# Where a kernel makes the token sums for a fast matrix product: in the convolution stage, or inside the two merges that come later

## The chip, the cores and the metric

One core of one Trainium2 chip. Five engines work on it side by side, each through its own instructions in order: TensorE (PE, matmuls; PEld is its weight load), VectorE (DVE), ScalarE (ACT), GpSimd (POOL) and SyncE (SP). DMAs are issued from the queues of SP, POOL and ACT. The metric is the device time of one execution, in microseconds (us); lower is better.

## The reference, cut to what matters

The program is one step of a backbone for 2048 sample tokens and 128 prompt tokens of width 1024. One input projection feeds three branches: A (short convolution on q, k, v, then a gated DeltaNet scan in both directions), B (spatial gating) and C (Fourier mixing). Each branch is projected to the model's width and multiplied by a sigmoid gate that is itself a projection of the same tokens; the three products are added, projected once more and added to the tokens.

```python
proj = jnp.einsum('btd,de->bte', xn, w_in)
qkv, beta, dec, z_a, u_b, v_b, z_b, x_c, z_c, gates = jnp.split(proj, points, axis=-1)
qkv = short_conv(qkv, conv_w).astype(jnp.float32)
...
br = jnp.stack([o_a, o_b, o_c], axis=2)
pb = jnp.einsum('btnw,nwd->btnd', br, w_branch)
gt = jax.nn.sigmoid(gates.reshape(B, T, N_BRANCH, D_MODEL))
merged = jnp.einsum('btnd,btnd->btd', gt, pb)
return jnp.einsum('btd,de->bte', merged, w_out), s_f, s_b
```

## The kernel before, in words

**Numbers.** Every matrix is held as two 16-bit parts, a high and a low one (`whi`, `wlo`; `x` has both in one tile), and a product is three matmuls that add in one PSUM bank. `mm`, the helper that records every matmul, is line 161, so nearly all matmuls have that line. The normalised tokens stay in SBUF as four quarters, `XQ` (`x_4` to `x_7` in the lists of instructions), plus `xp` for the prompt.

**Weights.** A block of 128 columns is read into one of two staging buffers `wst` (line 195, queue of SP), squared on ACT for its scale (L209), the sum cast on DVE (L175, `wscb`) and spread over the partitions by a small matmul with `ones`; DVE makes the scale from it (L183 to L187, `winv` L220), ACT writes the high part (L222) and DVE the low part (L223), which frees the staging buffer. A list `wlist` holds the order; `getw` and `weight_step` walk through it ahead of use.

**Stages.** First the tokens are normalised and transposed and `z_a` is projected. Then comes the convolution stage: twelve column blocks of q, k and v (`ct`), each a projection of all tokens in five pieces (four of 512, one of 128), copied by ACT into `raw` (L784), three passes of DVE over 2178 columns (L793 to L795), a sigmoid on ACT and a product on POOL (L799). Beside it run the decays of the scan (`decays`, DVE L584 to L624, then L689 and L690 per chunk; its loads are L673 on SP's queue). From the seventh block on, two weights a block are needed, as `w_out` and `w_branch` are converted and stored too (`keep`, L752). Behind it come the branches B and C, with the scan's preparation and the scan itself beside them, and then three merges: branch B (`merge(1, ...)`), branch C (`merge(2, ...)`) and branch A (`last_merge`).

**The merges.** `merge` goes through eight column blocks (`db`), each in two halves of the tokens (`h0` = 0 with two pieces, `h0` = 1024 with three). A piece is the gate's product (24 matmuls of 512 columns), its sigmoid on ACT into a buffer `sg` (L1530), the branch's product (12 matmuls) and their product on DVE (L1536, or L1539 in the second merge, where POOL then adds the row of the merge before, L1540). The scan's steps are interleaved: copies into T and R on POOL (L1022, L1024), key products on POOL (L1128, L1131), and splits into two 16-bit parts on ACT and DVE (L1065, L1066).

**The token sums.** The last merge's gate products use a scheme that needs fewer products, and it takes sums and differences of the token quarters in their place. `token_sums` (lines 701 to 738) makes them: for each of 2 x 4 parts of the tokens four steps, each of which makes one result. `whole` (L717, POOL) adds the two parts of a token quarter into a buffer `sg`; L723, L730 and L734 (DVE) and L727 (POOL) add and subtract; `pair_out` splits the result again into a buffer `st`, high part on ACT (L708), low part on DVE, or POOL for the fourth step (L709), and POOL's queue stores it (L711), two steps late. There are four buffers `sg` and three `st`; the merges take their `sg` from the same four. The four results go to DRAM (`xs`, 8.4 MB) and are read back by the last merge alone.

Before, 12 of the 32 steps are taken in the first three convolution blocks, one behind each piece of 512 tokens, and 20 behind the loop over the blocks.

**What sets the order.** The program is written as a stream of instructions, and a scheduler then sorts the instructions of each engine by priority (the order of writing, except where `high_priority` lifts one) and by a timeline of its own. So an instruction that is written later can stand earlier, and one edit changes the order in many places.

## Time and profile before

| | us |
|---|---|
| median of three runs | 2239.32 (2233.18 to 2240.04) |
| the profiled execution | 2242.02 |
| its span, first to last instruction | 2240.2 |
| PE busy | 2134.1 (95%) |
| DVE busy | 1443.1 (64%) |
| ACT busy | 1047.8 (47%) |
| POOL busy | 827.7 (37%) |
| mean granted clock of PE | 0.984 |

Busy time counts an engine's instructions, not its waits, nor the issue of DMAs from its queue. A row of a view of groups reads: line, engine, operation, what it writes <- what it reads, shapes, count, busy time, mean of one in ns, then the engine's idle time just before these instructions and who ended it. A row of the order of time reads: start, duration, then the same names, and in brackets the idle time before and who ended it. A row of waits reads: who waited for whom, total, times, the longest. "PEq", "SPq" and so on are an engine's queue.

### The profile page before, as it was taken

What the parts mean: (1) busy time and instruction counts of PE and PEld (TensorE: products, weight loads), DVE (VectorE), ACT (ScalarE), POOL (GpSimd) and SP (SyncE); (2) the same over time, 40 slices, a digit from 0 to 9 for tenths busy, and PEclk for the clock granted to TensorE, in tenths of its full rate; (3) what the DMA queues carried; (4) which work ended last, traced back from release to release, by engine and by line L of the source; (5) the groups of instructions that cost most, each with busy time, mean ns of one, the idle gap of its engine ahead of it and who ended that gap; (6) DMA issues with size and microseconds to landing.
All of it is one profiled execution on the core that took longest, in us unless ns stands there. A gap on an engine that the chain in (4) does not pass through costs nothing. (4 is left out here: it accounts for less than half of the span.)

```text
span 2240.2 us, 42450 instructions
## 1 busy us (share of the span) xinstructions
PE 2134.1 (95%) x15878; PEld 1227.4 (55%) x15878; DVE 1443.1 (64%) x3250; ACT 1047.8 (47%) x2394; POOL 827.7 (37%) x972
## 2 busy tenths in 40 slices
PE   7998978999899999899999999999999999999998
PEld 3564433445555567788755565565555445444443
DVE  5748989558888877735565555675565455444553
ACT  3634754546565656334464444665554332222331
POOL 1445467322243332233312232345453323433443
PEclk9999989999999999999999999999999999999999
DMA  8423944448787765424475555676664856564542
GB/s 273 159 83 119 313 158 148 145 134 253 230 289 227 215 199 154 106 83 143 130 223 172 161 167 175 201 231 207 202 204 153 255 165 201 179 223 149 167 142 86
DMA packets 333625, 404.94 MB, mean 181 GB/s; under 512 B 41345, under 2 KB 240106, under 8 KB 330602
## 3 DMA queue, kind: packets, MB, share of 16 engines
q1 hardware_dynamic: 311114, 327.36, 48.1%
q0 software_dynamic: 15248, 59.66, 7.3%
q10 hardware_dynamic: 7056, 15.21, 1.8%
q8 instruction: 125, 2.05, 0.4%
q14 instruction: 82, 0.67, 0.1%
HBM read 259.83 MB, written 142.30 MB: 180 GB/s over the span
## 5 line engine op out<-in xcount | busy, mean ns | idle before, releaser
L161 PE MATMUL b<-x,whi 128*128 128x512 f16 x3008 | 908.2, 382 | 5.5 <-DVE sg L1539 2.5
L161 PE MATMUL b<-x,wlo 128*128 128x512 f16 x1504 | 574.2, 382 | 0.0
L161 PEld LDWEIGHTS <-whi 128*128 128x128 f16 x3776 | 346.5, 98 | 338.1 <-issue 35.6
L161 PEld LDWEIGHTS <-wlo 128*128 128x128 f16 x1888 | 185.6, 98 | 180.7 <-issue 13.8
L161 PE MATMUL b<-big,bhi 128*128 128x512 f16 (+1 forms) x960 | 251.7, 348 | 2.9 <-ACT big L1500 1.5
L161 PE MATMUL b<-big,blo 128*128 128x512 f16 (+1 forms) x480 | 163.4, 348 | 0.0
L161 PEld LDWEIGHTS <-x 128*128 128x128 f16 x2176 | 131.3, 98 | 43.6 <-issue 4.2
L161 PEld LDWEIGHTS <-bhi 128*128 128x128 f16 x960 | 86.8, 98 | 74.9 <-issue 3.7
L161 PE MATMUL b<-x,m 128*128 128x512 f16 x528 | 114.8, 379 | 0.0
L799 POOL TENSOR_TENSOR cy<-cy,raw 128x545 f32<-128x545 f32 (+1 forms) x48 | 72.4, 1547 | 109.6 <-ACT raw L798 109.6
L1022 POOL COPY T<-ES 32x256 f16<-32x256 f16 x68 | 31.4, 462 | 208.1 <-DMA ES<-ei 202.5
L209 ACT ACTIVATE wlo<-wst 128x1024 f16<-128x1024 f32 (+1 forms) x64 | 64.2, 1003 | 93.6 <-DMA wst<-in_w_in_dram 64.0
L223 DVE SCALAR_TENSOR_TENSOR wlo<-wst,wsc,whi 128x1024 f16<-128x1024 f32 (+1 forms) x64 | 91.1, 1426 | 19.3 <-ACT whi L222 18.8
L222 ACT ACTIVATE whi<-wst,wsc 128x1024 f16<-128x1024 f32 (+1 forms) x64 | 69.7, 1093 | 64.2 <-DVE wsc L186 57.9
L161 PE MATMUL b<-whi,x 128*128 128x128 f16 x1024 | 90.7, 219 | 0.0
L1128 POOL TENSOR_TENSOR skn<-skn,ed 128x512 f32<-128x512 f32 x34 | 36.3, 1067 | 144.8 <-DMA skn<-kv 128.5
L175 DVE CAST wscb<-wss 128x1 bf16<-128x1 f32 x101 | 15.3, 152 | 111.9 <-ACT wlo L209 74.3
L161 PE MATMUL b<-wlo,x 128*128 128x128 f16 x512 | 87.4, 219 | 0.0
L161 PEld LDWEIGHTS <-m 128*128 128x128 f16 x528 | 51.1, 98 | 61.4
L161 PE MATMUL b<-x,zhi 128*128 128x512 f16 x256 | 78.7, 383 | 0.1
L161 PE MATMUL b<-v4hi,x 128*128 128x512 f16 x256 | 78.5, 383 | 0.1
L1660 POOL TENSOR_TENSOR mrow<-mrow,sg 128x512 f32<-128x512 f32 (+1 forms) x40 | 46.5, 1165 | 82.2 <-DVE sg L1659 73.9
(483 smaller groups left out, 4475.6 us busy)
## 6 DMA issues: line engine op xcount, KB each, us to landing
wst<-in_w_in_dram SPq DMA_DIRECT2D x56, 512.0 KB, 4.7
qkv<-cy POOLq DMA_DIRECT2D x12, 1089.0 KB, 5.7
st<-br SPq DMA_DIRECT2D x48, 256.0 KB, 3.5
mrow<-mrg SPq DMA_DIRECT2D x16, 576.0 KB, 4.5
mrg<-mrow POOLq DMA_DIRECT2D x16, 576.0 KB, 3.7
dc<-dec SPq DMA_DIRECT2D x17, 512.0 KB, 4.6
kq<-qkv SPq DMA_DIRECT2D x34, 256.0 KB, 4.2
kv<-tok POOLq DMA_DIRECT2D x17, 512.0 KB, 5.6
```

What stands on the lines that cost most here:

```text
L161: PE.matmul(out, l, r, start=start, stop=stop)
L175: V.tensor_copy(sb16, ss)
L209: A.activation(w.lo, st, AF.Square, accum_out=ss)
L222: w.made = A.activation(w.hi, st, AF.Copy, scale=s)
L223: V.scalar_tensor_tensor(w.lo, st, s, w.hi, ALU.mult, ALU.subtract)
L799: G.tensor_tensor(y[:, c0:c1], y[:, c0:c1], raw[:, 1 + c0:1 + c1], ALU.mult)
L1022: G.tensor_copy(T16[rows(a0, b), :, :, b], ES[0:32, :, 2 * a0 + b, :, wT])
L1128: G.tensor_tensor(h3(kn_), h3(kn_), bc(ed[:, d, t, :], P), ALU.mult)
L1660: G.tensor_tensor(mr, mr, sg, ALU.add)
```

## The change

The calls of the token sums in the convolution stage go, both the one behind a piece and the loop behind the blocks. In their place `merge` takes four steps, which is one whole part, before the second half of column blocks 1 to 4, in both of its calls: 2 x 4 x 4 = 32 steps. The two stores that are still owed at the end are issued behind the second merge.

```diff
                 pace.tick(tn / 100)
-                if ct < 3 and tn == 512:
-                    next(sums)
                 if ct > 4:
                     weight_step()
...
     pace.drain()
-    with tc.issue_after(dlast[0].ins):
-        for _ in sums:
-            pass
     a1.close()
...
                 if each is not None and (n == 0 or db > 3):
                     next(gates, 0)
+                if h0 and 0 < db < 5:
+                    for _ in range(4):
+                        next(sums)
                 for t0, tn in tbs:
...
     inv_ = merge(2, False, inv_, finish_delta, then=(0, 17))
+    for _ in sums:
+        pass
     cs_.close()
```

Lines behind the first edit have numbers two lower in the changed program, those behind the second five lower, and those behind the third two lower again; from the last merge on they are the same.

DVE at the decays, at the start of the convolution stage. `tok` holds the decays; `sg` and `st` are the sums' buffers. Before:

```order
L597 TENSOR_SCALAR tok_1779<-tok_1779 128x136
L598 RECIPROCAL tok_1779<-tok_1779 128x136
L730 TENSOR_TENSOR sg_2147<-sg_2091,sg_2147 128x512
L709 TENSOR_TENSOR st_2150<-sg_2089,st_2150 128x512
L599 TENSOR_TENSOR tok_1779<-tok_1779 128x136
L600 TENSOR_SCALAR tok_1779<-tok_1779 128x136
L601 TENSOR_TENSOR tok_1779<-tok_1779 128x136
L602 TENSOR_TENSOR tok_1779<-tok_1779 128x136
L709 TENSOR_TENSOR st_2196<-sg_2147,st_2196 128x512
L734 TENSOR_TENSOR sg_2243<-sg_2243,sg_2147 128x512
L603 SCALAR_TENSOR_TENSOR tok_1779<-tok_1779 128x136
L610 SCALAR_TENSOR_TENSOR tok_1779<-tok_1779,al_1783 128x68 x2
```

Now:

```order
L597 TENSOR_SCALAR tok_1779<-tok_1779 128x136
L598 RECIPROCAL tok_1779<-tok_1779 128x136
L599 TENSOR_TENSOR tok_1779<-tok_1779 128x136
L600 TENSOR_SCALAR tok_1779<-tok_1779 128x136
L601 TENSOR_TENSOR tok_1779<-tok_1779 128x136
L602 TENSOR_TENSOR tok_1779<-tok_1779 128x136
L603 SCALAR_TENSOR_TENSOR tok_1779<-tok_1779 128x136
L610 SCALAR_TENSOR_TENSOR tok_1779<-tok_1779,al_1783 128x68 x2
```

Four instructions of the sums have left the chain of the decays, whose last row PE's prefix sums read.

DVE at about the seventh and eighth column block, between the low part of one weight (L223) and the cast of the next (L175). `cy` is the convolution. Before:

```order
L220 TENSOR_TENSOR winv_2957<-wsc_2952,xsc_305 128x1
L223 SCALAR_TENSOR_TENSOR wlo_2917<-wst_2875,wsc_2952,whi_2916 128x1024
L730 TENSOR_TENSOR sg_4208<-sg_4201,sg_4208 128x512
L709 TENSOR_TENSOR st_4211<-sg_4199,st_4211 128x512
L734 TENSOR_TENSOR sg_4220<-sg_4220,sg_4208 128x512
L793 TENSOR_SCALAR cy_3015<-raw_2845,pc_111 128x2178
L175 CAST wscb_3062<-wss_3060 128x1
L794 SCALAR_TENSOR_TENSOR cy_3015<-raw_2845,pc_111,cy_3015 128x2178
L709 TENSOR_TENSOR st_4216<-sg_4208,st_4216 128x512
L723 TENSOR_TENSOR sg_4229<-sg_4227,sg_4229 128x512
L795 SCALAR_TENSOR_TENSOR cy_3015<-raw_2845,pc_111,cy_3015 128x2178
```

Now:

```order
L220 TENSOR_TENSOR winv_2875<-wsc_2870,xsc_305 128x1
L223 SCALAR_TENSOR_TENSOR wlo_2835<-wst_2793,wsc_2870,whi_2834 128x1024
L791 TENSOR_SCALAR cy_2933<-raw_2763,pc_111 128x2178
L175 CAST wscb_2980<-wss_2978 128x1
L792 SCALAR_TENSOR_TENSOR cy_2933<-raw_2763,pc_111,cy_2933 128x2178
L793 SCALAR_TENSOR_TENSOR cy_2933<-raw_2763,pc_111,cy_2933 128x2178
```

The five instructions of the sums are gone; the rest stands in the same order.

POOL in the first merge, where the first group comes in. `skn`, `kn`, T and R belong to the scan, `x_4` to `x_7` are the token quarters. Before:

```order
L1131 TENSOR_TENSOR kn_1874_14145<-skn_14111,kn_1874_14145 128x512
L1128 TENSOR_TENSOR skn_14393<-skn_14393,ed_1399 128x512
L1022 COPY T_1513_10755<-ES_10761 32x8x32 x2
L1024 COPY R_1512_10753<-ES_10761 32x8x32 x4
L1131 TENSOR_TENSOR kn_1909_14427<-skn_14393,kn_1909_14427 128x512
L1128 TENSOR_TENSOR skn_14689<-skn_14689,ed_1399 128x512
```

Now:

```order
L1123 TENSOR_TENSOR skn_14195<-skn_14195,ed_1399 128x512
L717 TENSOR_TENSOR sg_14154<-x_4_93 128x512
L717 TENSOR_TENSOR sg_14156<-x_5_94 128x512
L717 TENSOR_TENSOR sg_14162<-x_6_95 128x512
L1017 COPY T_1449_10531<-ES_10537 32x8x32 x2
L1019 COPY R_1448_10529<-ES_10537 32x8x32 x4
L727 TENSOR_TENSOR sg_14154<-sg_14162,sg_14154 128x512
L717 TENSOR_TENSOR sg_14173<-x_7_96 128x512
L711 DMA xs_1436<-st_14159 256x1x512
L1126 TENSOR_TENSOR kn_1853_14229<-skn_14195,kn_1853_14229 128x512
L711 DMA xs_1438<-st_14165 256x1x512
L711 DMA xs_1437<-st_14169 256x1x512
```

Three sums now stand ahead of the copies into T and R, and two more, with a store, ahead of the key product (L1126, before L1131); each waits for a free `sg`.

## The prediction, made before the changed kernel was run

> **What bounds the kernel now.** On the page TensorE (PE) is the busiest engine in nearly every slice of the span, so time can come only from the stretches in which it stands still or runs slowly. I read the waits of PE over the whole run first, then the busy times by stage. Around the change there are two places: the convolution stage, from which the token sums leave (about 150 to 448 us), and column blocks 1 to 4 of the first two merges, into which they go. Busy times of the convolution stage (stretch, length, then PE, PEld, DVE, ACT, POOL busy with counts, granted clock, DMA share, GB/s), and PE's waits in it:
>
> ```profile
> 150.00:213.00 63.00, 55.86 (x566) 32.38 (x564) 45.88 (x57) 23.89 (x43) 38.90 (x45) 0.95 0.37 117
> 213.00:287.00 74.00, 74.00 (x418) 36.43 (x416) 70.81 (x63) 53.63 (x68) 29.40 (x27) 1.00 0.78 266
> 287.00:396.00 109.00, 86.28 (x427) 39.67 (x426) 101.77 (x97) 54.73 (x86) 76.77 (x85) 0.91 0.44 150
> 396.00:448.00 52.00, 51.07 (x296) 25.48 (x296) 28.36 (x54) 28.61 (x42) 13.08 (x19) 1.00 0.47 151
> ...
> PE b L161 <- DVE wscb L175: 23.6, 6, 8.2
> PE b L161 <- DVE tok L610: 7.1, 1, 7.1
> ```
>
> The token sums run in the first and third stretch. In the second and fourth, which do the same convolution without them, PE is busy 74.00 of 74 and 51.07 of 52 us. In the third PE lacks 22.7 us while DVE is busy 101.77 of 109 us and POOL 76.77; in the first it has one hole of 7.1 us. Every wait named is one on a small DVE instruction: the cast that starts a weight's scale (L175), and the last step of the decays (L610).
>
> Idle time is not the whole loss, because PE comes back slow. Two pairs of rows of PE's order of time, before and behind the hole at 179 us, and the matmuls of 287 to 396 us by shape:
>
> ```profile
> 178.30 0.59 PE L161 MATMUL b<-x,whi 128*128 128x512 f16 x2
> 178.73 0.38 PE L161 MATMUL b<-x,wlo 128*128 128x512 f16 x1
> ...
> 188.36 0.63 PE L161 MATMUL b<-x,wlo 128*128 128x512 f16 x1
> 188.79 0.63 PE L161 MATMUL b<-x,whi 128*128 128x512 f16 x1
> ...
> L161 PE MATMUL b<-x,whi 128*128 128x512 f16 x232 | 74.0, 401 | 0.0
> L161 PE MATMUL b<-x,wlo 128*128 128x512 f16 x116 | 46.3, 399 | 0.0
> L161 PE MATMUL b<-xp,whi 128*128 128x128 f16 x48 | 4.3, 219 | 0.0
> L161 PE MATMUL b<-xp,wlo 128*128 128x128 f16 x24 | 4.2, 219 | 0.0
> ```
>
> Before the hole two matmuls start within 0.43 us, 0.215 each; behind it one start takes 0.43. At 0.215, the 348 long matmuls and the 72 short ones (a quarter of the columns, 18 long ones) need 366 x 0.215 = 79 us. The stretch took 109: **30 us lost**. Behind the 7.1 us hole, some 4 us at half speed lose 2 more: **9 us**.
>
> **What the change takes out.** How a late cast comes about, by the order of time on DVE, POOL, SP and ACT:
>
> ```profile
> 306.38 4.44 DVE L752 TENSOR_TENSOR oinv<-winv,xsc 128x1 f32<-128x1 f32 x1
> 310.71 1.35 POOL L717 TENSOR_TENSOR sg<-x 128x512 f32<-128x512 f16 x1
> 310.75 5.81 DVE L223 SCALAR_TENSOR_TENSOR wlo<-wst,wsc,whi 128x1024 f16<-128x1024 f32 x1
> 311.82 2.44 POOL L799 TENSOR_TENSOR cy<-cy,raw 128x545 f32<-128x545 f32 x2
> 316.59 0.38 SPq L195 DMA_DIRECT2D wst<-in_w_out_dram  x1
> 320.45 1.06 ACT L209 ACTIVATE wlo<-wst 128x1024 f16<-128x1024 f32 x1 [0.30 <-DMA wst<-in_w_out_dram]
> 325.23 0.14 DVE L175 CAST wscb<-wss 128x1 bf16<-128x1 f32 x1
> ...
> 395.44 0.16 DVE L752 TENSOR_TENSOR oinv<-winv,xsc 128x1 f32<-128x1 f32 x1
> 395.52 1.28 DVE L223 SCALAR_TENSOR_TENSOR wlo<-wst,wsc,whi 128x1024 f16<-128x1024 f32 x1
> ```
>
> L752 and L223 took 10.3 us here and take 1.44 when POOL leaves them alone (395.44, 395.52). L223 frees the weight's staging buffer, so the next read is issued only at 316.59, its square ends at 321.5, and the cast then stands behind sums and a convolution until 325.23: PE's 8.2 us hole. Without sums this chain is about 9 us earlier, and the cast has less ahead of it. The work that leaves, grouped over 150 to 410 us:
>
> ```profile
> L709 DVE TENSOR_TENSOR st<-sg,st 128x512 f16<-128x512 f32 x24 | 28.1, 1180 | 1.8 <-ACT st L708 1.8
> L734 DVE TENSOR_TENSOR sg<-sg,sg 128x512 f32<-128x512 f32 x8 | 10.6, 1321 | 0.0
> L730 DVE TENSOR_TENSOR sg<-sg,sg 128x512 f32<-128x512 f32 x8 | 10.4, 1300 | 1.2 <-POOL sg L727 1.2
> L723 DVE TENSOR_TENSOR sg<-sg,sg 128x512 f32<-128x512 f32 x8 | 7.3, 918 | 3.9 <-POOL sg L717 3.9
> ...
> L717 POOL TENSOR_TENSOR sg<-x 128x512 f32<-128x512 f16 x32 | 46.4, 1452 | 8.7 <-DVE sg L730 4.9 <-DVE wsc L183 2.1 <-DMA sz<-sg 1.6
> L711 POOL DMA_DIRECT2D xs<-st x30 | 21.2, 714 | 26.6 <-DVE st L709 11.5 <-DVE wsc L183 7.5 <-DVE wscb L175 2.1
> L727 POOL TENSOR_TENSOR sg<-sg,sg 128x512 f32<-128x512 f32 x8 | 11.9, 1486 | 2.8 <-DVE sg L723 2.8
> L709 POOL TENSOR_TENSOR st<-sg,st 128x512 f16<-128x512 f32 x8 | 10.8, 1344 | 5.2 <-ACT st L708 5.2
> ...
> L708 ACT CAST st<-sg 128x512 f16<-128x512 f32 x32 | 19.5, 614 | 37.7 <-DMA xs<-st 18.3 <-DVE sg L734 9.6 <-issue 3.7
> ```
>
> That is 56.4 us of DVE, 69.1 of POOL plus about 23 for 32 DMA issues (0.71 each), 19.5 of ACT. None is PE work; what comes back is the loss it causes. Not all of the 39 us is its doing:
>
> ```profile
> PE b L161 <- DVE wscb L175: 3.2, 1, 3.2
> ...
> PE b L161 <- DVE wscb L175: 2.0, 1, 2.0
> ...
> SPq L1224 <- DVE dc L689: 7.6, 1, 7.6
> ...
> 288.92 1.04 ACT L209 ACTIVATE wlo<-wst 128x1024 f16<-128x1024 f32 x1
> 291.57 1.13 ACT L708 CAST st<-sg 128x512 f16<-128x512 f32 x2
> ```
>
> PE's first two holes behind 287 us (at 280 to 296 and at 296 to 310 us: 3.2 and 2.0 of the 23.6) belong to weight reads that stood on SP's queue behind a load waiting for the decays (L1224). The square that ends the first starts at 288.92, before the burst's first sum on ACT (291.57); SP's order there is unchanged. With their share of the slow restarts (7.3 x 5.2/23.6 = 1.6) that is 6.8 us that stay. Left: 30 - 6.8 = 23.2, and 9 of the first place. The ends are 0 and 39 us. I take the upper part, since the two stretches without sums run full, one with DVE busy 70.81 of 74; 3 us stay in the burst's place, as other late reads, and 1.5 at the decays. **Term 1: -28 us** (20.2 + 7.5).
>
> **What it adds.** Eight groups of four steps. By the means above a group costs DVE 3 x 1.18 + 1.32 + 1.30 + 0.92 = 7.1 us, POOL 4 x 1.45 + 1.49 + 1.34 = 8.6 and 2.9 for four issues, ACT 2.5: for one merge 28, 46 and 10 us. There, blocks 1 to 4 of the first and of the second merge, and the scan's splits:
>
> ```profile
> 1184.80:1353.00 168.20, 167.98 (x1538) 100.21 (x1536) 94.82 (x261) 73.23 (x168) 46.57 (x76) 1.00 0.55 164
> 1497.50:1673.50 176.00, 173.78 (x1577) 104.28 (x1576) 109.88 (x290) 97.10 (x278) 89.84 (x114) 1.00 0.69 209
> ...
> L1066 DVE SCALAR_TENSOR_TENSOR S<-S,S x23: 679/776/1515, 1191.2 to 1672.6; 128x512 f16<-128x512 f32 x23
> ```
>
> DVE comes to 123 of 168 and 138 of 176 us, POOL to 93 and 136, ACT to 83 and 107: all have room. What can reach PE is a wait in a queue. On POOL a sum waits for one of four `sg` buffers, and behind it stand the copies into T and R and the key products for the next scan step, in the second merge the row additions that free `sg` too. On ACT a sum's copy waits for one of three `st` buffers (18.3 us of DMA waits in the ACT row above), and behind it stand the gate's sigmoid and the scan's copies. PE is covered by three PSUM banks: while a sigmoid is late, it can do the branch product and the next gate, (12 + 24) x 0.215 = 7.7 us. The cost per step lies between 0 (nothing that PE waits for is removed, so no gain) and what a step cost in the burst, 23.2/20 = 1.16 us, 37 in all. The nearest row is the second merge against the first: 43 us more of POOL, 15 of DVE and 24 of ACT, for 2.0 more of PE idle. So 2 us a merge, and 1 for the second, whose POOL gets fullest. **Term 2: +5 us.** The 32 DMAs of 256 KB add about 8 MB where the DMA share is 0.55 and 0.69; hidden. The sums' results are read only by the last merge, more than 100 us after the last group; hidden.
>
> -28 + 5 = -23. The profiled execution took 2242.0 us (span 2240.2), 2.7 above the median of 2239.3; I count from the median: **2216 us**.
>
> **A rule against it.** The Trainium skill (SBUF — State Buffer, "Who interferes with whom") says a DVE instruction with two SBUF inputs and a GpSimd instruction that reads SBUF exclude each other, the later one waiting until the earlier is done. The trace agrees that L223 stood while POOL worked, but 5.81 - 1.28 = 4.5 us is longer than any one POOL row there. By the rule a hit in the merges costs at most one POOL instruction, and the time would be that of rival 1; by the row, that of rival 2.
>
> **Rivals.** (1) *The merges take it back.* POOL's sums meet the scan's splits (L1066: S, v, u, 69 in 489 us, 6 in a block of 42). With POOL held 8.6 of 42 us, 1.2 splits a group are hit; at 1.45 us each, all passed on to PE, 8 groups lose 14 us: -28 + 14 = -14, 2225. For it: S splits already go from 0.68 to 1.5; against: PE lost 0.22 us in all of the first stretch. (2) *Slower.* A hit costs what L223 lost, 4.5 us, because POOL starts one sum after the other: 8 x 1.2 x 4.5 = 43 us, +15, 2254. It decides from 28/8 = 3.5 us a group on. For it: the burst; against: 7.7 us of cover. (3) *The convolution stays held* by weight reads on SP's queue, so only half of term 1 returns: -14 + 5, 2230. For it: the holes at 287 us; against: 396 to 448. (4) *Nothing shows*, since the scheduler sorts the whole program anew and loses elsewhere what it wins: 2239. That the sums stay where they were is out: the order shows them in the merges.
>
> **How the numbers follow.** Forecast 0.68 (2203 to 2224), rival 1 0.13, rival 3 0.08, rival 2 0.07, rival 4 0.04. The range, 2203 to 2231, takes in rivals 1 and 3 and leaves out both ends. A difference under 0.3% (6.7 us) cannot be told from no change. Faster: 0.68 + 0.09 + 0.06 = 0.83; within: 0.09; slower: 0.08.
>
> **What would show it.** Right: in the convolution stage PE's waits on L175 fall from 23.6 to under 9 us and the 7.1 on L610 to under 2; L223 there stays below 2.5 us; the stage ends about 28 us earlier; PE's idle time in the merges' blocks 1 to 4 rises from 2.4 to under 8 us. Wrong: holes of 3 us and more behind T, R or `sg` in the merges, or holes at the weights that stay without sums on DVE.

## The result: 11 to 19 us faster where 23 were forecast

| | before | changed |
|---|---|---|
| median, us | 2239.68 (2233.18 to 2243.20, six runs) | 2228.34 (2224.63 to 2230.22, six runs) |
| the profiled execution | 2242.02 | 2224.63 |
| its span | 2240.2 | 2222.9 |
| ratio | | 0.9950, 95% interval 0.9933 to 0.9966 |

The changed kernel was timed twice more, on other chips, each time beside the kernel before: 0.9917 (0.9888 to 0.9946) and 0.9934 (0.9919 to 0.9949). By these ratios it is 11, 19 and 15 us faster. The forecast of 23 (a ratio of 0.990) is inside the second interval and outside the other two; 2228 is inside its range. The two profiled executions differ by more than the medians of the first timing, 17.4 us, because the profiled execution of before lay above its median and that of the change was the fastest of its six. What follows compares spans.

**The convolution stage came out as forecast, and a little better.** Busy times by stretch in the change (what stood at 396 us before stands at 364 now), and all waits of PE from 150 to 436 us:

```profile
150.00:213.00 63.00, 63.00 (x622) 36.30 (x620) 30.62 (x48) 28.15 (x46) 3.14 (x11) 1.00 0.39 128
213.00:287.00 74.00, 74.00 (x402) 35.76 (x400) 56.63 (x55) 48.82 (x62) 39.97 (x33) 1.00 0.68 241
287.00:364.00 77.00, 69.91 (x377) 33.50 (x376) 42.75 (x70) 35.00 (x56) 24.89 (x32) 0.98 0.41 136
364.00:416.00 52.00, 52.00 (x301) 25.81 (x299) 26.83 (x47) 28.14 (x42) 12.41 (x16) 1.00 0.36 120
```

```profile
PE b L161 <- DVE wscb L175: 7.1, 3, 5.5
```

PE is busy 63.00 of the first 63 us (55.86 before), the wait for the decays is gone, and the casts (L175) hold PE for 7.1 us in place of 23.6.

**The two merges took much of it back.** To measure stages, take the first matmul on `bdp` (151.3 us before, 150.8 now; the convolution stage begins), the first on `v4hi` (branch B begins), and the stores of the merges' rows (`mrg<-mrow`): the first merge issues its 16 from SP's queue, the second its 16 from POOL's. First and last start of each, before and changed:

```profile
L161 PE MATMUL b<-v4hi,x x256: 376/379/634, 468.2 to 590.0; 128*128 128x512 f16 x128
L1547 SPq DMA_DIRECT2D mrg<-mrow x16: 319/327/382, 1148.1 to 1470.1; - x16
L1547 POOL DMA_DIRECT2D mrg<-mrow x16: 557/628/638, 1491.0 to 1807.0; - x16
```

```profile
L161 PE MATMUL b<-v4hi,x x256: 376/379/634, 435.9 to 558.4; 128*128 128x512 f16 x128
L1545 SPq DMA_DIRECT2D mrg<-mrow x16: 319/337/597, 1115.9 to 1441.6; - x16
L1545 POOL DMA_DIRECT2D mrg<-mrow x16: 571/616/651, 1461.5 to 1791.2; - x16
```

| stage | before | changed | difference |
|---|---|---|---|
| up to the convolution stage | 151.3 | 150.8 | -0.5 |
| convolution stage | 316.8 | 285.0 | -31.8 |
| branches, to the first row's store | 679.9 | 680.0 | 0.1 |
| merge 1, first store to last | 322.0 | 325.7 | 3.7 |
| between the merges' stores | 20.9 | 19.9 | -1.0 |
| merge 2, first store to last | 316.0 | 329.7 | 13.7 |
| rest | 433.2 | 431.7 | -1.5 |
| span | 2240.2 | 2222.9 | -17.4 |

Term 1 was -28 and measured -31.8. Term 2 was +5 for both merges; they are 3.7 and 13.7 us longer, 17 together. Waits of PE in merge 2, before (all six rows) and changed (the first five of nine):

```profile
PE b L1213 <- ACT o L1209: 3.2, 4, 1.1
PE b L161 <- DVE sg L1539: 2.5, 1, 2.5
PE b L161 <- ACT sg L1530: 0.8, 1, 0.8
PE b L161 <- DVE S L1066: 0.5, 1, 0.5
PE b L161 <- DVE R L1038: 0.5, 1, 0.5
PE b L161 <- ACT S L1065: 0.4, 1, 0.4
```

```profile
PE b L161 <- DVE S L1061: 4.2, 3, 2.6
PE b L161 <- ACT sg L1528: 4.1, 1, 4.1
PE b L161 <- DVE sg L1537: 2.4, 1, 2.4
PE b L161 <- ACT S L1060: 2.2, 1, 2.2
PE b L161 <- DVE u L1061: 1.6, 2, 1.3
```

PE now waits 6.4 us for the scan's state S, 0.9 before. The longest single hole, 4.1 us behind a sigmoid (ACT `sg`, 0.8 before), is of another kind. It ends at 1784.0 us, 122 us behind the last instruction of the sums (a store at 1662.0), and the sigmoid stood on ACT behind a copy for the last merge (L1495) that waited 2.2 us for its load. That hole is 2.5 to 5.7 us in the four executions whose merge 2 has the change's groups (changed, a1, a2, e2 below) and 0.8 to 2.1 in the seven without groups there, so some of the price arises at the end of the merge. What moves it there was not tried.

Busy times from first to last store of merge 2 (stretch, length, then PE, PEld, DVE, ACT, POOL), before and changed:

```profile
1491.00:1807.00 316.00, 308.15 (x2463) 174.74 (x2462) 186.25 (x479) 158.44 (x424) 134.48 (x157) 0.99 0.66 204
```

```profile
1461.50:1791.20 329.70, 311.62 (x2464) 176.86 (x2463) 223.88 (x501) 166.37 (x438) 180.43 (x196) 0.98 0.66 208
```

PE stands still for 18.1 us in place of 7.9 and is busy 3.5 us longer for the same number of matmuls; together that is the 13.7. In a1 the same 13.7 are 13.3 of standing still and 0.4 of longer busy time. POOL's busy times in such rows count the issue of DMAs from its own queue, other than was said of busy times above; the sums' 16 stores in merge 2 are 11.2 us of them.

The split of S on DVE, ten times in that merge, before and changed (count, busy us, mean ns):

```profile
L1066 DVE SCALAR_TENSOR_TENSOR S<-S,S 128x512 f16<-128x512 f32 x10 | 10.4, 1038 | 3.9 <-ACT S L1065 3.7
```

```profile
L1061 DVE SCALAR_TENSOR_TENSOR S<-S,S 128x512 f16<-128x512 f32 x10 | 13.2, 1323 | 4.7 <-ACT S L1060 4.6
```

### The profile page after: what moved, and what is told of

Read it like the earlier page. It is cut to its first block, busy times and chain, and to the rows that moved or that the text cites. A ratio compares the mean times of both kernels' runs of the same rounds, so it can differ in the third digit from the quotient of the medians.

```text
span 2222.9 us, 42461 instructions
## 1 busy us (share of the span) xinstructions
PE 2129.5 (96%) x15878; PEld 1227.4 (55%) x15878; DVE 1409.8 (63%) x3250; ACT 1043.7 (47%) x2392; POOL 839.9 (38%) x972
## 5 line engine op out<-in xcount | busy, mean ns | idle before, releaser
L797 POOL TENSOR_TENSOR cy<-cy,raw 128x545 f32<-128x545 f32 (+1 forms) x48 | 80.2, 1696 | 191.3 <-ACT raw L796 191.3
L223 DVE SCALAR_TENSOR_TENSOR wlo<-wst,wsc,whi 128x1024 f16<-128x1024 f32 (+1 forms) x64 | 85.5, 1339 | 35.1 <-ACT whi L222 34.7
L1017 POOL COPY T<-ES 32x256 f16<-32x256 f16 x68 | 32.5, 478 | 165.2 <-DMA ES<-ei 159.2
L175 DVE CAST wscb<-wss 128x1 bf16<-128x1 f32 x101 | 15.4, 153 | 96.8 <-ACT wlo L209 63.3
```

The source lines that it names most:

```text
L175: V.tensor_copy(sb16, ss)
L223: V.scalar_tensor_tensor(w.lo, st, s, w.hi, ALU.mult, ALU.subtract)
L797: G.tensor_tensor(y[:, c0:c1], y[:, c0:c1], raw[:, 1 + c0:1 + c1], ALU.mult)
L1017: G.tensor_copy(T16[rows(a0, b), :, :, b], ES[0:32, :, 2 * a0 + b, :, wT])
```

## Experiments

Eighteen runs were made, in five sets, each on one chip beside the kernel before: e1, e2, e4, e5; then a1, e9, e7, e12; e13, e5 again, e10, e6; e14, e15, e16; and a2, e17, e18. The table gives for each its ratio to before, and from its profiled execution the stages' lengths as above.

| kernel | ratio (95%) | convolution | merge 1 | merge 2 |
|---|---|---|---|---|
| before | 1 | 316.8 | 322.0 | 316.0 |
| changed | 0.9950 (0.9933 to 0.9966) | 285.0 | 325.7 | 329.7 |
| e1 stores only | 0.9890 (0.9871 to 0.9909) | 285.8 | 324.0 | 314.6 |
| e2 sums twice | 1.0059 (1.0036 to 1.0083) | 318.5 | 326.8 | 330.7 |
| e4 merge 2 in blocks 0 to 3 | 0.9928 (0.9903 to 0.9953) | 285.0 | 329.0 | 329.2 |
| e5 all in merge 1 | 0.9894 (0.9872 to 0.9916) | 284.6 | 330.3 | 321.6 |
| a1 changed, again | 0.9917 (0.9888 to 0.9946) | 281.4 | 327.1 | 329.7 |
| e9 no sums, stores held | 0.9889 (0.9856 to 0.9921) | 285.8 | 325.2 | 322.4 |
| e7 additions on DVE | 0.9916 (0.9884 to 0.9949) | 286.1 | 332.0 | 320.9 |
| e12 all on POOL | 0.9943 (0.9926 to 0.9961) | 286.3 | 322.9 | 334.4 |
| e13 all in merge 1 and on POOL | 1.0151 (1.0130 to 1.0172) | 284.9 | 392.0 | 315.5 |
| e5 again | 0.9891 (0.9869 to 0.9913) | 281.2 | 335.6 | 317.6 |
| e10 in the third branch | 1.0012 (0.9998 to 1.0026) | 285.8 | 327.4 | 315.8 |
| e6 finer steps | 0.9940 (0.9917 to 0.9963) | 286.6 | 325.5 | 334.7 |
| e14 merge 2 without POOL | 0.9872 (0.9851 to 0.9892) | 280.0 | 322.7 | 327.9 |
| e15 stores on SP | 0.9927 (0.9902 to 0.9952) | 284.6 | 326.7 | 335.7 |
| e16 all in merge 1, stores on SP | 0.9919 (0.9902 to 0.9936) | 286.6 | 339.7 | 316.7 |
| a2 changed, third time | 0.9934 (0.9919 to 0.9949) | 285.5 | 328.3 | 329.5 |
| e17 merge 2 on DVE | 0.9877 (0.9860 to 0.9894) | 279.9 | 326.3 | 325.0 |
| e18 e14 again | 0.9922 (0.9910 to 0.9935) | 285.3 | 325.3 | 332.8 |

Each stage length is one execution's. How much that says is seen where the same work ran several times: merge 2 with the change's groups took 329.7, 329.7, 329.5 and 330.7 us (changed, a1, a2, e2); merge 1 with no groups took 322.0, 324.0 and 327.4 (before, e1, e10), and merge 2 with none 316.0, 314.6, 315.5, 315.8, 316.7, 317.6 and 321.6. Merge 1 with the change's four groups took 322.7 to 328.3 us (changed, a1, a2, e2, e14, e17, e18), so what it pays is hardly clear of that scatter.

### Is it the sums' work, or the new order?

**e1: only the stores.** The sums are left out; the parts are stored as they are, so the last merge computes from other numbers.

```diff
-                x21, x22 = whole(k, tb), whole(4 + k, tb)
-                V.tensor_tensor(x22, x21, x22, ALU.add)
-                pair_out(0, x22, k, tb, V)
-                yield 1
...
+                for i, (p_, q_) in enumerate(((0, 0), (0, 1), (1, 0), (1, 1))):
+                    G.dma_start(sD[i][:, :, k, tb:tb + 512], XQ[p_][q_][:, :, k, tb:tb + 512])
+                    yield 1
```

> As the changed kernel, but the additions, subtractions and splits of the token sums are left out: each step only stores the token quarter as it is, by the same POOL queue, in the same number and size of stores, in the same groups of the two merges (so the last merge's gates are computed from wrong operands). Theory A, that the sums' work on POOL, DVE and ACT inside the merges costs PE the 14 us which the profiles show there: the convolution keeps its gain of about 31 us, the merges lose as little as before, and the time is 27 to 31 us under before (2209 to 2213). Rival B, that the loss in the merges comes from the new sorting of all instructions and not from the sums' work: the merges lose some 10 us again, and the time is 15 to 22 us under before. Rival C, that the stores (8 MB more of DMA traffic in the merges) are what costs: as the change, about 11 us under before.

Measured: 2220.4 us, 24 under the kernel before. The merges are as short as before (324.0 and 314.6), the convolution stage 31 us shorter. As it stands, 24 us is between theory A (27 to 31) and rival B (15 to 22). Less the 7.9 us by which its start was late, it would be 2212.5, 32 under the kernel before on its chip and on theory A's side. The stores depend on nothing that the merges make, and the scheduler put all 32 among the first instructions of POOL (51 to 139 us), beside the tokens' preparation; so this run has neither sums nor stores in the merges, and says nothing on rival C. The convolution stage starts at 159.2 in place of 151.3 us:

```profile
L161 PE MATMUL b<-bdp,x x256: 169/174/180, 159.2 to 173.4; 128*128 128x32 f16 x112, 128*128 128x16 f16 x16
```

**e9: no sums, stores held in the merges**, each behind a store of `mrow` and on its queue, which is SP's in merge 1 and POOL's in merge 2; the sums are left out as in e1.

```diff
+                    eng, behind = held_by[0]
+                    with tc.issue_after(behind):
+                        eng.dma_start(sD[i][:, :, k, tb:tb + 512], XQ[p_][q_][:, :, k, tb:tb + 512])
...
+                eng = SY if first else G
+                held_by[0] = eng, eng.dma_start(mD[db][:, h0:h0 + hn], mrow).ins
```

> The changed kernel with the sums' arithmetic left out; each store of a quarter (unsummed halves of x, so the last merge gets other numbers) now stands behind a store of mrow in the merges, so that none can slip into the start as in the run with stores alone. Theory A (the sums' arithmetic is what the merges pay for): merges as long as before, PE waits on the splits of S back to about 1 us, 28 to 32 us under the kernel before. Theory B (the moved loads and the order at the end of merge 2 are what is paid for, not the arithmetic): 15 to 22 us under.

Measured: 25 us under the kernel before, between the two theories; the start is whole again. Merge 2 is 322.4, 7 us less than in the change and 6 more than before. That is just over the longest merge 2 without groups (321.6), so whether the stores alone cost anything is not shown, and neither is that they cost nothing.

**e2: the sums made where they were and once more in the merges**, into memory that nobody reads.

```diff
-    sums = token_sums()
+    sums, sums2 = token_sums(sD), token_sums([dram(f"xt{i}", [P, 2, 4, 1024], F16) for i in range(4)])
...
+                if h0 and 0 < db < 5:
+                    for _ in range(4):
+                        next(sums2)
```

> The kernel before, with the sums where they were, and made a second time in the eight groups of the merges, into DRAM that nobody reads: the added part alone. Theory A: PE's idle and slow time in the merges rises by 10 to 18 us and the time is 10 to 18 us over before (2250 to 2258). Rival B: the rise depends on the sorting, so it need not come near 14; anything from 0 to 25. If the rise is under 5 us, the loss belongs to the convolution's new end and not to the groups.

Measured: 14.5 us over the kernel before by the medians, 18.7 by the spans; merge 1 is 4.8 and merge 2 14.7 us longer. So the price in the merges is the same whether or not the convolution stage is rid of its sums: it isn't a trade between the two. That falls to theory A. As nothing was taken from the convolution stage here, this run shows best that merge 2's price is the groups' doing.

### Does the place count?

**e4: merge 2's groups one block earlier**, away from block 4, where the last merge's gate rows are summed on DVE as well.

```diff
-                if h0 and 0 < db < 5:
+                if h0 and (0 < db < 5 if first else db < 4):
```

> The changed kernel with the second merge's four groups in column blocks 0 to 3 in place of 1 to 4, so that none stands in block 4, where the sums of the last gate's rows (L460, L462 on DVE) begin. Theory A, in the form that the group in block 4 met those sums and cost 7 of the 14 us: 5 to 7 us under the changed kernel, about 2222, with PE's loss in blocks 4 and 5 of the second merge back at 2 us. Rival B: within 3 us of the changed kernel, the loss turning up elsewhere.

Measured: merge 2 took 329.2 us, as in the change; the ratio (0.9928) lies among the change's own three. The collision in block 4 is not the cause.

**e6: the same steps in smaller bits**, one before each piece of 512 tokens.

```diff
-                if h0 and 0 < db < 5:
-                    for _ in range(4):
-                        next(sums)
                 for t0, tn in tbs:
+                    if 0 < db < 5 and tn == 512:
+                        next(sums)
```

> The changed kernel with its four steps of a group no longer in one place ahead of the second half of a block, but one ahead of each 512-token piece of blocks 1 to 4 of both merges: the same work in smaller bits. Theory A with the hit on S by the group as a whole (9 to 10 us of waits behind S in merge 2): waits on S under 4 us, merge 2 318 to 323 us long, 3 to 8 us faster than the change. If the load alone counts: within 3 us of the change.

Measured: merge 2 334.7 us, 5 longer than in the change; the ratio (0.9940) is no better. A miss: spreading does not help.

**e5: all eight groups in merge 1**, two to a block.

```diff
-                if h0 and 0 < db < 5:
+                if first and 0 < db < 5:
```

> The changed kernel with all eight groups in the first merge, one before each half of column blocks 1 to 4, none in the second. Theory A, that the loss grows with what POOL and DVE already have to do: the second merge loses no more than before (11 of the 14 us return), the first loses 4 to 8, so 2216 to 2221. Rival B: no different from the change by more than 3 us. Rival D, that groups so dense (one in 21 us) fill POOL: the first merge loses 15 us or more and the time is 2232 or above.

> The kernel with all eight groups in merge 1, sums on DVE and POOL as in the change, once more on the chip of its neighbours here. Theory A: 20 to 26 us under the kernel before and 0 to 6 us behind the one with all sums on POOL. Theory C: as the change, 11 to 18 us under.

Measured, on two chips: 24 us under the kernel before (0.9894 and 0.9891), as theory A had it, and more than the change's 11 to 19. But A also put the second of them 0 to 6 us behind e13, which came out 58 us slower than it. Merge 1 pays 8 and 14 us for eight groups; merge 2, which has none, was 5.6 and 1.6 longer than before.

**e10: all steps in the third branch**, where DVE and POOL were freest.

```diff
+                if q < 16:
+                    for _ in range(2):
+                        next(sums)
                 pace.tick(1.5 * qn)
...
-                if h0 and 0 < db < 5:
-                    for _ in range(4):
-                        next(sums)
```

> No sums in the merges: two of the 32 steps stand in each of four column turns of the third branch, in all four of its groups (DVE 159 of 266 us busy there, POOL 74). Theory A (the sums cost where DVE or POOL release PE late; both are freer here): 1 to 5 us in that stage, merges 367 and 315 us long as before, 24 to 30 us under the kernel before. Theory C: some 15 us in that stage too, 11 to 18 us under.

Measured: no faster than before (1.0012). Branches to first row took 712.4 us, 32 more, although the merges are free of sums. PE's waits in that stage, the longest of them:

```profile
PE b L851 <- issue: 6.4, 1, 6.4
PE b L161 <- ACT xc L1414: 5.1, 2, 4.6
PE b L161 <- DVE wsc L183: 4.3, 1, 4.3
PE b L161 <- POOL T L1017: 4.3, 1, 4.3
```

Single holes of 4 to 6 us, behind PE's own issue, ACT, DVE and POOL: a low busy share (DVE 60%, POOL 28% before) did not make room. A miss for both theories: A had 1 to 5 us there, C some 15.

### Which engine?

**e7: the 32 additions of the two parts on DVE** in place of POOL. **e12: the mirror**, all sums and low parts on POOL.

```diff
-            G.tensor_tensor(t_, h_, l_, ALU.add)
+            V.tensor_tensor(t_, h_, l_, ALU.add)
```

```diff
-                V.tensor_tensor(x22, x21, x22, ALU.add)
-                pair_out(0, x22, k, tb, V)
+                G.tensor_tensor(x22, x21, x22, ALU.add)
+                pair_out(0, x22, k, tb, G)
...
-                V.tensor_tensor(x12, x12, x11, ALU.subtract)
+                G.tensor_tensor(x12, x12, x11, ALU.subtract)
```

> The changed kernel with the 32 additions of hi and lo (1.31 us each on POOL, 41 us in all) made by DVE instead, about 0.9 us each by the nearest row, so 29 us more on DVE. Theory A1 (POOL's reading stretches DVE's splits, S from 1.04 to 1.32 us in merge 2): the splits of S back towards 1.04 us, the waits on S to 2 or 3 us, 3 to 6 us faster than the change. Theory A2 (what stands ahead of the split in DVE's own queue is what delays it): more stands there, 3 to 10 us slower than the change.

> The changed kernel with all sums and low halves on POOL, the mirror of the run with the additions on DVE: DVE is rid of 36 us (24 low halves of 0.82, 16 sums of 1.0), POOL has 54 us more (24 of 1.41, 16 of 1.27). Theory A1 (POOL's reading stretches DVE's splits): splits of S longer than 1.32 us in merge 2, 3 to 10 us slower than the change. Theory A2 (DVE's own queue): waits on S to 2 or 3 us, 3 to 6 us faster than the change.

Busy times from first to last store of merge 2, as shown above for the change, in e7 and in e12:

```profile
1471.20:1792.10 320.90, 307.51 (x2464) 175.27 (x2462) 217.24 (x516) 164.34 (x438) 161.04 (x180) 0.99 0.69 213
```

```profile
1461.50:1795.90 334.40, 315.04 (x2477) 178.38 (x2476) 196.48 (x472) 161.38 (x433) 201.56 (x219) 0.98 0.64 200
```

With POOL 19 us freer, merge 2 is 9 us shorter; with POOL 21 us fuller, 5 longer, though DVE was rid of 27. That is theory A1's side in merge 2, but not by its mechanism alone: the splits of S, which A1 had longer than 1.32 us in e12, took 0.97 (1.10 in e7).

```profile
L1061 DVE SCALAR_TENSOR_TENSOR S<-S,S 128x512 f16<-128x512 f32 x10 | 9.7, 974 | 3.4 <-ACT S L1060 3.1
```

In merge 1 it is the other way round: 332.0 with the additions on DVE, 322.9, as short as without sums, with everything on POOL. That is one execution each, and with the change's own division e14 below took 322.7. e7 as a whole is no faster than the change on its chip (2225.57 against 2221.49), where A1 had 3 to 6 us. Its profiled execution won 8.8 us in merge 2 against a1's and lost 4.9 in merge 1, 4.7 in the convolution stage, for a reason told below that has nothing to do with the sums, and 3.8 in the branches.

**e13: all eight groups in merge 1, all on POOL**, the sum of what had cost least in each place.

```diff
-                if h0 and 0 < db < 5:
+                if first and 0 < db < 5:
...
-                V.tensor_tensor(x22, x21, x22, ALU.add)
-                pair_out(0, x22, k, tb, V)
+                G.tensor_tensor(x22, x21, x22, ALU.add)
+                pair_out(0, x22, k, tb, G)
```

> All eight groups in merge 1 (one ahead of each half of blocks 1 to 4), and every sum and low half on POOL. With all sums on POOL, merge 1 was 366 us long with four groups (367 in the kernel before), and merge 2, where POOL adds up mrow as well, 335 (315 before). Theory A (each merge pays on the engine that is loaded there; POOL is free in merge 1, 102 of 367 us busy): merge 1 with eight groups 367 to 373 us, merge 2 315 to 321, 24 to 32 us under the kernel before. Theory C (merge 1 was short by chance, sums cost some 2 us a group wherever they are): 14 to 20 us under.

Measured: 33 us over the kernel before, where A had 24 to 32 under. Merge 1 took 392.0 us. The stretch with the groups:

```profile
1156.00:1398.00 242.00, 197.93 (x1594) 117.76 (x1592) 122.26 (x288) 93.30 (x207) 169.97 (x196) 0.87 0.52 160
```

POOL is busy 170 of 242 us there, no more than 70%, the issue of its stores included, yet PE stands still for 44. Over the whole of merge 1 PE's busy time rose too, from 317.10 to 343.93 us, as it ran at a lower clock (0.87 in this stretch). POOL works in order, and the scan's copies into T and R and its key products stand between the sums; that each late one makes the next scan step late is how I read it. Four groups on POOL alone had cost 0.9 us in this merge (in one execution), eight cost 70: nothing that could be read off the first four.

**e14: merge 2's groups wholly off POOL**, arithmetic on DVE and stores on SP's queue; merge 1 as in the change. **e17: the same with the stores left on POOL's queue.** **e18: e14 again, a2: the change again**, all three on one chip.

```diff
-        for tb in (0, 512):
+        for tb, E, Q in ((0, G, G), (512, V, SY)):
...
-                G.dma_start(*owed.pop(0))
+                Q.dma_start(*owed.pop(0))
...
-            G.tensor_tensor(t_, h_, l_, ALU.add)
+            E.tensor_tensor(t_, h_, l_, ALU.add)
...
-                G.tensor_tensor(x21, x11, x21, ALU.subtract)
+                E.tensor_tensor(x21, x11, x21, ALU.subtract)
...
-                pair_out(3, x12, k, tb, G)
+                pair_out(3, x12, k, tb, E, Q)
```

In e17 the second line's `SY` is `G`.

> The changed kernel with POOL kept out of merge 2's four groups: their hi+lo additions, x21's difference and the fourth low half are made by DVE, and their stores go by SP's queue (30 us less on POOL there, some 25 us more on DVE). Theory P (in merge 2 the sums cost by POOL: 315 us without them, 329 with 47 us more on POOL, 335 with 72 more, 321 with 27 more): merge 2 316 to 320 us, 18 to 24 us under the kernel before. Theory Q (by DVE's queue): 330 us or more, 5 to 12 us under.

> The changed kernel with all arithmetic of merge 2's four groups on DVE and their stores left on POOL's queue. Theory P2 (POOL's arithmetic costs merge 2 about 8 us, and the stores on SP's queue cost 6: 321 us with the additions on DVE, 336 with the stores on SP, 328 with both): the part of merge 2 up to its last but one store 318 to 323 us long (316 before, 330 in the change), and 4 to 8 us faster than the same change with the stores on SP, 6 to 11 us faster than the change. Theory Q (DVE's queue as dear as POOL's): 326 us or more there, within 4 us of the change.

> The kernel with merge 2's groups on DVE and their stores on SP's queue, once more, beside the change and beside its twin with the stores on POOL's queue. If its 29 us under the kernel before came from the merges alone, they stand again (24 to 32 under, 8 to 14 us faster than the change). If a good part came from more of its executions having POOL's products ahead of the decays: 17 to 24 under, 2 to 7 us faster than the change.

> The changed kernel once more, on the chip of its two neighbours here: 11 to 19 us under the kernel before. Its executions should fall into two groups some 6 to 9 us apart, by whether POOL's four products cy (L797) near 250 us run ahead of DVE's decay products (5.7 us; the weights' hole at 287 us is then 0.4 us) or across them (12.2 us; hole 5.5 us). If the spread is only noise, the executions lie evenly.

Merge 2 took 325.0 us in e17, 327.9 and 332.8 in e14 and e18: 325 is between the 323 of the one theory and the 326 of the other, so POOL's share of the 13.7 us may be smaller than e7 alone suggested. One execution each does not say more, as e14 and e18, one kernel, differ by 4.9. By theory P, with SP's stores thought free, e14 had 316 to 320; that failed. What did go as A1 says is the wait on S. PE's waits in merge 2 of e17 (nine rows):

```profile
PE b L161 <- ACT sg L1528: 5.7, 1, 5.7
PE b L161 <- DVE R L1033: 4.5, 3, 3.4
...
PE b L161 <- DVE S L1061: 0.2, 1, 0.2
```

```profile
L1061 DVE SCALAR_TENSOR_TENSOR S<-S,S 128x512 f16<-128x512 f32 x10 | 9.0, 897 | 4.4 <-ACT S L1060 4.2
```

Without POOL's sums beside it the split of S takes 897 ns (1323 in the change), and PE hardly waits for it. But other waits have come up in its place.

By the medians e14 is 30 us under the kernel before, e18, the same kernel, 17; e17 28 under and 12 under the change on its chip. Not all of that is the merges: in the profiled executions of e14 and e17 the convolution stage was 5 us shorter than in those of e18 and a2 (280 against 285), for a reason told below. The two groups of times that were expected of a2 didn't show: its six executions lie evenly from 2225 to 2235. e17 beats the change and the kernel before, and so do both runs of e5 beat the kernel before; between e5, e14 and e17 these runs don't decide. e18 was timed beside the change and is no more than 1 us faster by the medians, where both of its theories had more.

**e15 and e16: the stores on SP's queue**, in the change and with all groups in merge 1.

```diff
-                G.dma_start(*owed.pop(0))
+                SY.dma_start(*owed.pop(0))
...
-            G.dma_start(*o_)
+            SY.dma_start(*o_)
```

> The changed kernel with nothing but the sums' 32 stores moved from POOL's queue to SP's (each holds POOL for 0.70 us, 11 us in each merge). Theory P, linear in POOL's time: merge 2 some 3 us shorter than in the change (326), within 5 us of the change in all. If the stores' place on POOL were what counts (merge 2 was 7 us longer with stores alone): 6 to 8 us faster than the change. If loads behind a waiting store on SP's queue come late: slower than the change by 5 or more, with PE waits behind DMA.

> All eight groups in merge 1, and their stores on SP's queue (22 us less on POOL in blocks 1 to 4 of merge 1, where POOL is busy 120 of 177 us). Theory P: merge 1 4 to 6 us shorter than the 373 to 378 us with the stores on POOL, 25 to 31 us under the kernel before. If POOL's stores don't count: within 3 us of that kernel, 20 to 26 us under.

Measured: each store had held POOL for 0.70 us, but taking them off gained nothing. Merge 2 is 335.7 us in e15 (329.7), merge 1 339.7 in e16 (330.3 and 335.6), and e16 is 6 us slower than e5 by the ratios. Moved to SP a store waits there for its sum (SP's queue stood 15 us in all at these stores in merge 2 of e15), and the loads of weights and rows behind it wait too; that this is the cause was not shown.

**a1: the change on another chip**, with e7, e9 and e12.

> The changed kernel itself, unaltered, beside the next kernels on one chip. Its profiled execution was the fastest of its six, so its stages are read a second time here. Every theory: 10 to 16 us under the kernel before; the convolution stage about 31 us shorter; the two merges 10 to 16 us longer, most of it in the second. If the second merge is as long here as in the kernel before, the 13 us read in the first profile were that execution's own.

Its merges cost 5.1 and 13.7 us, near the 3.7 and 13.7 of the first profile: that reading was not one execution's chance.

Not tried: buffers of their own for the sums. So whether the shared `sg` and `st` buffers have a part in merge 2's price stays open.

## Why the forecast was off

- **Term 1, -28 us: right.** Measured -31.8, -35.4 and -31.3 in three executions of the change. Its parts: the hole at the decays and its slow restart are gone whole (9 us by the prediction's own count, forecast 7.5); the other 22.8 of 31.8 came back in the burst's place (forecast 20.2). That two early weight reads would stay late was right as well: holes of 5.5 and 1.4 us in place of 3.2 and 2.0. That only SP's order holds them was too simple: in a1, with the same order, the first of them was 0.4 us.
- **Term 2, +5 us: this step failed.** The prediction put "2 us a merge, and 1 for the second" and measured, in three executions of the change against the one of before, are 3.7 to 6.3 in merge 1 (where executions without groups differ by 5 among themselves) and 13.5 to 13.7 in merge 2: 17 to 20 us in place of 5. The sentence that carried it was "all have room", said of DVE at 138 and POOL at 136 of 176 us. Four-fifths busy is not room when the work between is a chain. The row that the size was taken from, merge 2 against merge 1 (43 us more of POOL for 2.0 us of PE), was work that the kernel's order already held; the next 46 us of POOL, with 38 of DVE and 8 of ACT, cost almost seven times as much.
- **The cover of 7.7 us** by PSUM banks did hold in blocks 1 to 4: in the change PE has no wait behind `sg` there, in either merge. But it covers gates and branch products, not the scan's matmuls, which stand in PE's own order. PE's holes in blocks 1 to 4 of merge 2 are single ones of 0.4 to 2.6 us behind S, u, v and o. In the last block, where ACT waits for the last merge's loads, a sigmoid did hold PE, for 4.1 us.
- **Rival 1 had the mechanism in part, and nearly the right sum.** It priced eight groups at 14 us of hits on the scan's splits; the merges cost 17 to 20. That its total of -14 lies between the measured 11 and 19 is partly luck, as term 1 gave 3 to 7 us more than it counted on. But its hits were to be spread over both merges, 1.45 us each. In merge 2 the stretch of the ten splits of S is 2.8 us in all (13.2 against 10.4), so most of the price is something else, waiting in queues among it. One hole shows both, in a1: the order of time of ACT, DVE and POOL around one split of S.

```profile
1637.85 1.26 DVE L462 SCALAR_TENSOR_TENSOR sg<-wst,scT,sg 128x256 f32<-128x256 f32 x1
1637.96 0.63 ACT L1060 ACTIVATE S<-S 128x512 f16<-128x512 f32 x1
1639.14 0.29 DVE L1033 SCALAR_TENSOR_TENSOR R<-b,R 32x128 f16<-32x128 f32 x1
1639.46 0.75 DVE L1537 SCALAR_TENSOR_TENSOR sg<-b,binv,sg 128x512 f32<-128x512 f32 x1
1640.12 0.68 DVE L709 TENSOR_TENSOR st<-sg,st 128x512 f16<-128x512 f32 x1
1640.29 1.64 POOL L1538 TENSOR_TENSOR mrow<-mrow,sg 128x512 f32<-128x512 f32 x1 [1.46 <-DVE sg L1537]
1640.72 1.75 DVE L1061 SCALAR_TENSOR_TENSOR S<-S,S 128x512 f16<-128x512 f32 x1
```

  ACT had its part of S ready at 1638.6. DVE came to it at 1640.7, behind four others, of which L709 is the sums'; then the split ran beside POOL's row addition and took 1.75 us in place of 0.9. PE stood still for 2.5 us. Of this hole only L709's 0.68 us are an instruction of the sums: the row addition and the three others are work of the kernel before, and that they meet the split here is an effect of the new order.
- **Rival 2** (4.5 us a hit, slower than before) did not come. **Rival 3** (weight reads hold the convolution stage) did not come either. **Rival 4** (lost elsewhere by new sorting): the stages between, and behind, moved by 0.1 and -1.5 us; in e1 new sorting did cost 7.9 us at the start.
- **What would show it.** L175 under 9 us: 7.1. L610 under 2: gone. L223 below 2.5 us in the convolution stage: at most 1.8 us (row below). Stage end 28 us earlier: 32. PE idle in blocks 1 to 4 of the merges, by the stretches of the prediction's rows, under 8 us: wrong, 3.9 in the first merge and 8.4 in the second. Of the signs for wrong, one came: the hole of 4.1 us behind `sg`, though in the last block.

```profile
L223 DVE SCALAR_TENSOR_TENSOR wlo<-wst,wsc,whi x14: 1282/1535/1822, 246.4 to 401.5; 128x1024 f16<-128x1024 f32 x14
```

- **What stays open.** Shown is that the groups make merge 2 longer by some 13 us (329.5 to 330.7 us in four executions with them, 314.6 to 321.6 in seven without), and that neither their place in the merge nor smaller bits help. Moving their additions off POOL (e7) or all their arithmetic (e17) clears most of the wait on S and gave back 8.8 and 4.7 us, in one execution each, the second no more than one kernel's merge 2 can differ by. How the 13 us divide among POOL's queue, DVE's, ACT's, the shared buffers, the stores and the loads at the end of the merge stays open.

## What to carry to other kernels

Work that was taken out of a stage where PE visibly starved gave back what the stretches without it had promised (31 to 35 us, forecast 28). What it costs in its new place is not read from busy shares: where in-order engines carry a chain that PE waits for, the price rose from 0.9 us for four groups to 70 for eight on the same engine, so price the move by the chain's links that stand behind the new work, and try one dose and the double of it. And look which engine is short in each place: here, by one execution each, all on POOL was cheaper than the additions on DVE in the first merge (322.9 against 332.0 us) and dearer in the second (334.4 against 320.9).

## What the runs showed of the hardware

**One convolution, two courses.** In four executions (a1, e5 again, e14, e17) the convolution stage took 280 to 281 us, in the 14 others without its sums 285 to 287, though a1, a2 and the change are one program. What sets them apart shows near 250 us. The first of POOL's four products of a column block (L797), in the change and in a1:

```profile
250.87 5.91 POOL L797 TENSOR_TENSOR cy<-cy,raw 128x545 f32<-128x545 f32 x1 [8.45 <-ACT raw L796]
```

```profile
248.91 1.36 POOL L797 TENSOR_TENSOR cy<-cy,raw 128x545 f32<-128x545 f32 x1 [8.45 <-ACT raw L796]
```

and DVE beside it, in the change and in a1:

```profile
250.01 2.36 DVE L689 TENSOR_TENSOR XB<-XB,tok 128x1024 f32<-128x1024 f32 x2
252.28 2.36 DVE L690 TENSOR_TENSOR XB<-XB,cst 128x1024 f32<-128x1024 f32 x2
254.55 1.23 DVE L689 TENSOR_TENSOR dc<-dc,tok 128x1024 f32<-128x1024 f32 x1
256.44 0.16 DVE L175 CAST wscb<-wss 128x1 bf16<-128x1 f32 x1 [0.67 <-ACT wlo L209]
```

```profile
251.81 1.77 DVE L689 TENSOR_TENSOR XB<-XB,tok 128x1024 f32<-128x1024 f32 x1 [2.54 <-DMA XB<-gamR]
```

In the change DVE had begun a run of five decay products at 250.01, and POOL's one product, 1.36 us alone, took 5.91, until 256.8, just behind the first gap in DVE's run (255.8 to 256.4). In a1 DVE had to wait 2.54 us for a load, and POOL went through. All four products took 12.2 us and 5.7; in each of the four short executions they took 5.7, in the 14 others 10.1 to 12.2. The sigmoid and the weight behind them are 4 us later, and PE's hole at 287 us is 5.5 in place of 0.4 us. In all four short executions DVE waited 2.5 to 3.0 us for that load: the stage was shorter where the load came in later. The Trainium skill (SBUF — State Buffer, "Who interferes with whom") says that a DVE instruction with two SBUF inputs contends with a GpSimd instruction that reads SBUF, for a shared port pair that is an exclusive lock; the trace agrees that the two hold each other up, but POOL's product was held through five DVE instructions in a row and not one (5.91 us), as L223 before had been held through several of POOL's (5.81 us).

**Half clock behind a short hole.** Stretches around two holes of 2.6 and 2.2 us in merge 2 of the change; the granted clock is the number before the last two:

```profile
1643.70:1647.10 3.40, 1.07 (x17) 0.92 (x17) 2.94 (x4) 0.55 (x1) 3.31 (x4) 1.00 0.93 283
1647.20:1650.50 3.30, 3.30 (x18) 2.02 (x17) 2.39 (x7) 2.12 (x6) 2.83 (x3) 0.50 0.94 311
...
1664.10:1667.50 3.40, 1.07 (x11) 0.61 (x9) 3.27 (x9) 1.88 (x9) 0.47 (x1) 1.00 0.49 157
1667.70:1671.00 3.30, 3.30 (x9) 1.19 (x8) 3.19 (x8) 0.61 (x2) 2.46 (x3) 0.50 0.50 159
```

After a stretch of 3.4 us in which PE was busy 1.07, it ran the next 3.3 us at half clock, a loss of some 1.7 us on top of each hole. The forecast had such a loss in term 1 and none in term 2. It does not come with every long merge: in the change PE's busy time in merge 2 rose by 3.5 us, in a1 by 0.4.
